# Output projection of the first block in two parts, the first between retention's steps

## The chip, the cores and the metric

The kernel runs on one core of a Trainium2 chip. A core has TensorE (PE, matrix products into PSUM), VectorE (DVE), ScalarE (ACT), GpSimd (POOL) and SyncE (SP, which issues most transfers), and they wait for each other by semaphores. The metric is the device time of one execution in microseconds (us); lower is better.

## The reference

All arithmetic is in float32: one sequence of 512 tokens, width 1024, runs through two layers of a first block, then through one layer of a second block that the change leaves alone. In each layer of the first block a mixer has three branches whose outputs are concatenated and projected:

```python
def hybrid_layer(x, ...):
    h = rms_norm(x, g_mix_pre)
    u = h @ w_in
    aq, ak, av, cu, rq, rk, rv, rg = jnp.split(u, SPLITS, axis=-1)
    y_att = chunk_attention(aq, ak, av, rel_bias)          # 384 wide, 6 heads
    y_conv = conv_module(cu, conv_w, conv_b, ...)          # 256 wide
    y_ret = retention(rq, rk, rv, rg)                      # 384 wide, 6 heads
    mix = jnp.concatenate([y_att, y_conv, y_ret], axis=-1) @ w_out   # 1024 x 1024
    x = x + rms_norm(mix, g_mix_post)
    h = rms_norm(x, g_mlp_pre)
    f = jnp.square(jax.nn.relu(h @ w_up)) @ w_down
    return x + rms_norm(f, g_mlp_post)
```

## The kernel before

Activations lie feature-major: a tile has 128 features on the partitions and the 512 tokens along it, so a width of 1024 is eight tiles. Each float32 operand is split into a high and a low part (`split`, `wload`: ACT rounds the high part, DVE subtracts), and a product is three products on PE, high by high, low by high, high by low (`mm3`). One unit of weights is 128 output features, 128 x 1024 numbers or 512 KB; 24 products of 512 columns belong to it. Units pass through three buffers `raw` for the load and four pairs `wh`, `wl` for the parts.

`gemm` takes units in turn. With `wide` = 4 its first four units advance together, with the contraction outermost, so that each input tile is used for four units as soon as it is there; later units go one by one. Behind each unit it may advance background work, written as generators: `pump_all` takes one or more steps of each.

`mixer` computes the input projection part by part in the order "card": convolution, attention, retention, gates. Behind the units of a part the branches run as background: a head of attention is a step of scores and softmax (eight score products on PE, of 512, 384, 256 and 128 columns, twice each) and a step of values; a head of retention the same without the softmax, with masks by POOL. In retention each pair of heads ends with a norm over 64 features: sums on PE against `hsel`, a reciprocal root on ACT and DVE, its broadcast by transposes on PE, two multiplications on DVE. The eight tiles `mix` are three of attention, two of convolution, three of retention. Then comes the output projection (wide 4) over all eight, whose results ACT copies out of PSUM (`e_out`); background work beside it is `bg2`, the projection of the second block's memory (products of 256 columns on PE, splits of its weights in halves of 512 columns). `post` takes the sum of squares, normalizes, adds to x and prepares the input of `mlp`, whose first gemm is again wide 4.

Nothing runs in the written order. `Plan` records every operation with a priority (its place, shifted by `ahead` or `filler`), and a list scheduler orders the recorded operations by a model of the engines' times and its slots (80 tiles `t`, 8 PSUM tiles `p`). `emit` then issues them in that order. So every instruction has the line of `emit` in the profile, L475, and groups are told apart by tile names: `p<-t,wh` and `p<-t,wl` are products with weights ("weight products" below), `p<-t` products of activations and of the memory, `p<-ident` transposes, `p<-ones` and `p<-hsel` sums over features.

## Time and profile before

| | us |
|---|---|
| median of 3 runs | 2514.57 |
| lowest and highest run | 2509.88, 2519.38 |
| span of the profiled execution, first to last instruction | 2510.5 |
| busy in it: PE, DVE, ACT, POOL | 2483.7, 1462.8, 946.0, 110.7 |

For the profiled execution the page gives its span and no other time. Matrix products are pipelined and their ends are modelled, so a busy PE may still be slowed by its clock or by loads of weights. The granted clock stands beside each stretch: 1.00 is 2.4 GHz, 0.50 is 1.2 GHz. The first layer's mixer ends and its up projection begins at about 280 us, the second layer's at about 913 us.

### The profile page before, as it was taken

What the parts mean: (1) busy time and instruction counts of PE and PEld (TensorE: products, weight loads), DVE (VectorE), ACT (ScalarE), POOL (GpSimd) and SP (SyncE); (2) the same over time, 40 slices, a digit from 0 to 9 for tenths busy, and PEclk for the clock granted to TensorE, in tenths of its full rate; (3) what the DMA queues carried; (4) which work ended last, traced back from release to release, by engine and by line L of the source; (5) the groups of instructions that cost most, each with busy time, mean ns of one, the idle gap of its engine ahead of it and who ended that gap; (6) DMA issues with size and microseconds to landing.
All of it is one profiled execution on the core that took longest, in us unless ns stands there. A gap on an engine that the chain in (4) does not pass through costs nothing.

```text
span 2510.5 us, 30038 instructions
## 1 busy us (share of the span) xinstructions
PE 2483.7 (99%) x11522; PEld 2033.4 (81%) x11522; DVE 1462.8 (58%) x2529; ACT 946.0 (38%) x1482; POOL 110.7 (4%) x214
## 2 busy tenths in 40 slices
PE   8999999999999999999999999999999999999998
PEld 7777888888887788788888888888878888888887
DVE  7985734545897579934565444456445555444445
ACT  4465532223346453322343222234455433322222
POOL 0011000000001100310000000000000000000000
PEclk9998999999999899999999999999999999999999
DMA  6441333233354234533313332265222243232232
GB/s 208 133 124 51 120 109 101 93 101 118 126 143 109 66 120 129 154 119 97 117 61 113 95 106 88 89 225 169 83 77 73 72 137 109 84 109 87 91 107 69
DMA packets 98160, 274.83 MB, mean 109 GB/s; under 512 B 13153, under 2 KB 20001, under 8 KB 98017
## 3 DMA queue, kind: packets, MB, share of 16 engines
q1 hardware_dynamic: 93184, 259.51, 33.1%
q0 software_dynamic: 4832, 13.41, 1.8%
q8 instruction: 90, 1.47, 0.2%
q14 instruction: 54, 0.43, 0.1%
HBM read 242.44 MB, written 19.94 MB: 105 GB/s over the span
## 4 chain that ended last, share of the span: by engine, by line
PE 95%; DVE 3%; ACT 1%; issue 1%; DMA 0%; POOL 0%; DVEq 0%; SPq 0%; ACTq 0%
PE p L475 95%; DVE t L475 2%; ACT t L475 1%; DVE wl L475 0%; ACT wh L475 0%; DMA raw<-in_mem_kv 0%; DVE s L475 0%; POOL t L475 0%; DMA t<-in_x 0%; ACT L475 0%; ACT s L475 0%; DVEq L1929 0%; SPq L475 0%; DVEq L475 0%; ACTq L475 0%
## 5 line engine op out<-in xcount | busy, mean ns | idle before, releaser
L475 PE MATMUL p<-t,wh 128*128 128x512 f32 (+1 forms) x6408 | 1994.4, 390 | 8.2 <-ACT wh L475 7.6
L475 PEld LDWEIGHTS p<-t,wh 128*128 128x128 f32 x6408 | 1201.8, 188 | 259.5 <-ACT wh L475 9.3
L475 PE MATMUL p<-t,wl 128*128 128x512 f32 x3204 | 1248.6, 390 | 1.2 <-DVE wl L475 1.1
L475 ACT ACTIVATE wh<-raw 128x1024 fp32r<-128x1024 f32 (+4 forms) x428 | 426.1, 1000 | 1203.4 <-PE p L475 802.1
L475 PEld LDWEIGHTS p<-t,wl 128*128 128x128 f32 x3204 | 603.3, 188 | 125.4 <-DVE wl L475 3.6
L475 DVE TENSOR_TENSOR wl<-raw,wh 128x1024 fp32r<-128x1024 f32 (+4 forms) x428 | 489.3, 1147 | 144.2 <-ACT wh L475 140.0
L475 DVE TENSOR_TENSOR t<-p,t 128x512 f32<-128x512 f32 (+5 forms) x388 | 238.4, 630 | 488.8 <-PE p L475 463.4
L475 DVE TENSOR_TENSOR t<-t 128x512 f32<-128x512 f32 (+10 forms) x688 | 360.0, 551 | 39.8 <-ACT t L475 32.3
L475 ACT ACTIVATE t<-t 128x512 f32<-128x512 f32 (+4 forms) x405 | 244.6, 617 | 124.9 <-DVE t L475 110.7
L475 PE MATMUL p<-t 128*128 128x256 f32 (+14 forms) x1200 | 233.8, 324 | 5.7 <-DVE t L475 3.6
L475 PEld LDWEIGHTS p<-t 128*128 128x128 f32 (+3 forms) x1200 | 165.5, 179 | 68.5 <-issue 28.6
L475 DVE TENSOR_TENSOR t<-t,p 128x512 f32<-128x512 f32 x104 | 71.7, 692 | 178.3 <-PE p L475 174.0
L475 ACT ACTIVATE t<-p 128x512 f32<-128x512 f32 (+7 forms) x290 | 130.2, 491 | 118.7 <-PE p L475 108.5
L475 DVE SCALAR_TENSOR_TENSOR t<-t,cols 128x512 fp32r<-128x512 f32 (+32 forms) x196 | 132.9, 712 | 4.3 <-ACT t L475 4.2
L475 DVE SCALAR_TENSOR_TENSOR t<-p,t 128x512 f32<-128x512 f32 (+1 forms) x84 | 57.4, 684 | 122.9 <-PE p L475 122.8
L475 ACT ACTIVATE t<-t,cols 128x512 fp32r<-128x512 f32 (+2 forms) x76 | 49.5, 671 | 29.4 <-DVE t L475 28.7
L475 PE MATMUL p<-ident,t 128*128 128x128 f32 x388 | 55.8, 281 | 1.3 <-DVE t L475 1.3
L475 ACT ACT_TABLE_LOAD x41 | 52.6, 1283 | 6.2 <-DMA t<-in_x 4.0
L475 PEld LDWEIGHTS p<-ident,t 128*128 128x128 f32 x388 | 46.9, 144 | 8.7 <-DVE t L475 1.7
L475 ACT ACTIVATE t<-t,s 128x256 f32<-128x256 f32 (+2 forms) x80 | 42.4, 531 | 19.6 <-DVE s L475 18.9
L475 DVE SCALAR_TENSOR_TENSOR t<-t 128x512 f32<-128x512 f32 (+1 forms) x72 | 45.0, 631 | 1.5
L475 DVE CUSTOM_DVE_ANT_0 t<-p,t 128x256 f32<-128x256 f32 (+2 forms) x80 | 34.5, 451 | 13.5 <-PE p L475 13.4
(57 smaller groups left out, 359.7 us busy)
## 6 DMA issues: line engine op xcount, KB each, us to landing
raw<-in_w_in SPq DMA_DIRECT2D x100, 512.0 KB, 3.7
raw<-in_f_in SPq DMA_DIRECT2D x88, 512.0 KB, 3.5
raw<-in_w_up SPq DMA_DIRECT2D x64, 512.0 KB, 3.5
raw<-in_w_down SPq DMA_DIRECT2D x64, 512.0 KB, 3.6
raw<-in_w_out SPq DMA_DIRECT2D x24, 512.0 KB, 3.6
raw<-in_f_down SPq DMA_DIRECT2D x32, 384.0 KB, 3.0
raw<-in_f_down SPq DMA_DIRECT2D x32, 320.0 KB, 2.8
t<-t SPq DMA_DIRECT2D x72, 128.0 KB, 2.3
```

Source lines behind the costliest of these rows:

```text
L475: fn(*args, **kw)
```

## The change

The output projection is done in two gemms. The first is over the first five tiles of `mix` (`EARLY = 5`: attention and convolution). It is recorded as soon as these five are there, one unit after the other, with one step of the remaining background (retention) behind each unit, and its results are copied from PSUM to `f` by ACT as before. The second, behind the last step of retention, is over the other three tiles, again one unit at a time, and DVE adds its results in PSUM to `f`. Each unit of weights is loaded in two pieces, 128 x 640 and 128 x 384. Products per unit are 15 and 9 in place of 24. The rest of the diff takes out comments and docstrings.

```diff
@@ -489,6 +489,7 @@
 
 
 TAIL, BACK = 4, 100
+EARLY = 5
 
 
 class Net:
...
@@ -1027,17 +1028,24 @@
 
         for i, kind in enumerate(self.ORDER):
             part(kind, 1 if i else 4)
+        while None in mix[:EARLY]:
+            self.pump_all(bg)
+
+        f = [None] * KT
+
+        def e_first(i, ps):
+            f[i] = self.T()
+            nc.scalar.activation(f[i], ps, AF.Copy)
+
+        def e_rest(i, ps):
+            nc.vector.tensor_tensor(f[i], f[i], ps, op=OP.add)
+
+        wo = d[f"w_out{l}"]
+        self.gemm([wo[i][:, :EARLY * P] for i in range(KT)], [self.split(m) for m in mix[:EARLY]], e_first, 1, bg,
+                  both=True)
         while bg:
             self.pump_all(bg)
-
-        f = [None] * KT
-
-        def e_out(i, ps):
-            f[i] = self.T()
-            nc.scalar.activation(f[i], ps, AF.Copy)
-
-        wo = d[f"w_out{l}"]
-        self.gemm([wo[i] for i in range(KT)], [self.split(m) for m in mix], e_out, 4, bg2, 1)
+        self.gemm([wo[i][:, EARLY * P:] for i in range(KT)], [self.split(m) for m in mix[EARLY:]], e_rest, 1, bg2, 1)
         self.finish(bg2)
         self.unpark()
         return self.post(f, f"norm_mix_post{l}", f"norm_mlp_pre{l}")
```

How the order moves, at three places. First PE in layer 0, behind the last unit of the gates. Rows are engine instructions by line, output and inputs, shape of the output, and how often one follows itself. Before, this is where the first weight product of the output projection stands, behind 64 rows of attention, retention and transposes:

```order
L475 MATMUL p<-t 128x256
L475 MATMUL p<-t 128x512
L475 MATMUL p<-t 64x512
L475 MATMUL p<-t 128x256
L475 MATMUL p<-t 128x128 x2
L475 MATMUL p<-t,wh 128x512
L475 MATMUL p<-t 128x384
L475 MATMUL p<-t 64x384
```

In the new order, six weight products come at the start of that stretch (here five rows between two heads' scores):

```order
L475 MATMUL p<-t,wh 128x512
L475 MATMUL p<-t,wl 128x512
L475 MATMUL p<-t,wh 128x512 x2
L475 MATMUL p<-t,wl 128x512
L475 MATMUL p<-t,wh 128x512
L475 MATMUL p<-t 128x512 x2
L475 MATMUL p<-t 128x384 x2
L475 MATMUL p<-t 128x256
```

and later each set of products of retention stands between weight products. Here the end of a set of values and the products behind it:

```order
L475 MATMUL p<-t 128x256
L475 MATMUL p<-t 64x256
L475 MATMUL p<-t 128x128
L475 MATMUL p<-t 64x128
L475 MATMUL p<-t,wh 128x512
L475 MATMUL p<-t,wl 128x512
```

So weight products moved from behind retention to between its sets. Second, PE in layer 0 between the output projection and the up projection, before, from the sums of squares (`ones`) over the transposes of the norm (`ident,s`, four) to the first product of the up projection:

```order
L475 MATMUL p<-ones,t 128x1 x6
L475 MATMUL p<-t 128x256 x12
L475 MATMUL p<-ones,t 128x1 x4
L475 MATMUL p<-t 128x256 x4
L475 MATMUL p<-ident,s 128x128 x2
L475 MATMUL p<-t 128x256 x7
L475 MATMUL p<-ident,s 128x128 x4
L475 MATMUL p<-t 128x256 x24
L475 MATMUL p<-t,wh 128x512
```

and now:

```order
L475 MATMUL p<-t,wh 128x512
L475 MATMUL p<-t 128x256 x32
L475 MATMUL p<-ones,t 128x1 x8
L475 MATMUL p<-t 128x256 x7
L475 MATMUL p<-ident,s 128x128 x4
L475 MATMUL p<-t 128x256 x9
L475 MATMUL p<-t,wh 128x512
```

The products of the memory (128x256) moved from behind the norm's transposes to ahead of them. Third, DVE in layer 0 at the same place, a part of its list ahead of the statistics of the norm (`TENSOR_SCALAR s<-p 128x4`). Before, it has the subtractions for weights (`wl`) and for the memory's weights (`t<-raw,t`) and the sums of squares (`t<-t`), and no additions out of PSUM:

```order
L475 TENSOR_TENSOR wl<-raw,wh 128x1024 x3
L475 TENSOR_TENSOR t<-t 128x512 x4
L475 TENSOR_TENSOR wl<-raw,wh 128x1024 x2
L475 TENSOR_TENSOR t<-t 128x512
L475 TENSOR_TENSOR wl<-raw,wh 128x1024
L475 TENSOR_TENSOR t<-raw,t 128x512 x2
L475 TENSOR_TENSOR t<-t 128x512
L475 TENSOR_TENSOR wl<-raw,wh 128x1024
```

and now, up to the statistics, with additions out of PSUM (`t<-t,p`) among them:

```order
L475 TENSOR_TENSOR t<-t,p 128x512
L475 TENSOR_TENSOR t<-raw,t 128x512
L475 TENSOR_TENSOR t<-t 128x512
L475 TENSOR_TENSOR t<-t,p 128x512
L475 TENSOR_TENSOR wl<-raw,wh 128x1024
L475 TENSOR_TENSOR t<-t 128x512
L475 TENSOR_TENSOR wl<-raw,wh 128x1024
L475 TENSOR_TENSOR t<-p,t 128x256
L475 TENSOR_TENSOR t<-raw,t 128x512 x2
L475 TENSOR_TENSOR t<-t 128x512
L475 TENSOR_TENSOR wl<-raw,wh 128x1024
L475 TENSOR_SCALAR s<-p 128x4
```

The eight additions joined the list that ends with the statistics.

## Rows read from the trace of the kernel before

**Rows 1.** The page: span, part 1 (busy us, share, instructions), part 4 (the chain).

```profile
span 2510.5 us, 30038 instructions
...
PE 2483.7 (99%) x11522; PEld 2033.4 (81%) x11522; DVE 1462.8 (58%) x2529; ACT 946.0 (38%) x1482; POOL 110.7 (4%) x214
...
PE 95%; DVE 3%; ACT 1%; issue 1%; DMA 0%; POOL 0%; DVEq 0%; SPq 0%; ACTq 0%
```

**Rows 2.** Windows: stretch and length, each engine busy (x), granted clock, DMA share, GB/s.

```profile
193.20:210.30 17.10, 16.99 (x46) 10.71 (x45) 5.62 (x13) 9.04 (x23) 4.26 (x16) 0.50 0.27 90
...
797.40:807.60 10.20, 9.43 (x23) 6.66 (x23) 6.73 (x25) 6.54 (x18) 1.72 (x5) 0.50 0.15 39
807.60:824.70 17.10, 17.10 (x78) 12.24 (x77) 13.07 (x29) 8.60 (x15) 2.75 (x5) 1.00 0.35 108
824.70:838.30 13.60, 13.60 (x34) 8.35 (x34) 4.09 (x11) 7.13 (x18) 4.15 (x16) 0.50 0.32 97
...
848.60:855.40 6.80, 6.80 (x21) 4.76 (x21) 2.72 (x5) 2.99 (x7) 1.61 (x6) 0.50 0.87 298
```

**Rows 3.** Windows: one head's score products twice, one head's value products.

```profile
166.73:169.35 2.62, 2.62 (x9) 1.29 (x7) 2.62 (x7) 2.34 (x5) 0.00 (x0) 1.00 0.23 53
195.12:199.62 4.50, 4.50 (x9) 2.28 (x8) 2.02 (x5) 1.75 (x4) 2.14 (x9) 0.50 0.35 117
210.22:211.62 1.40, 1.40 (x9) 1.22 (x10) 0.96 (x4) 1.35 (x4) 0.00 (x0) 0.98 0.00 0
```

**Rows 4.** Timeline of PE: start, length, instruction, count.

```profile
803.08 0.63 PE L475 MATMUL p<-t,wl 128*128 128x512 f32 x1
803.51 1.05 PE L475 MATMUL p<-t,wh 128*128 128x512 f32 x2
...
808.17 0.62 PE L475 MATMUL p<-t,wh 128*128 128x512 f32 x2
808.63 0.39 PE L475 MATMUL p<-t,wl 128*128 128x512 f32 x1
```

**Rows 5.** Timeline of PE: its waits beside retention, in brackets.

```profile
226.96 0.27 PE L475 MATMUL p<-t 128*64 128x128 f32 x1 [0.45 <-POOL t L475]
...
840.27 1.21 PE L475 MATMUL p<-t 128*128 128x512 f32 x5 [0.70 <-DVE t L475]
...
859.91 0.27 PE L475 MATMUL p<-t 128*64 128x128 f32 x1 [0.45 <-POOL t L475]
```

**Rows 6.** DMA issues: count, KB each, median us from issue to landing.

```profile
raw<-in_mem_kv SPq DMA_DIRECT2D x8, 512.0 KB, 4.0
```

**Rows 7.** Groups by form, ACT, 189 to 280 us: busy, mean ns, idle before.

```profile
L475 ACT ACTIVATE t<-t 128x512 fp32r<-128x512 f32 x4 | 2.5, 622 | 2.8 <-DVE t L475 2.8
```

**Rows 8.** Windows: last retention transposes to the up projection, both layers.

```profile
236.23:279.76 43.53, 43.30 (x230) 37.23 (x229) 22.18 (x36) 20.86 (x34) 0.74 (x1) 1.00 0.42 140
868.27:912.70 44.43, 43.76 (x228) 37.20 (x227) 21.84 (x32) 20.44 (x32) 1.09 (x2) 1.00 0.41 129
```

**Rows 9.** Timeline of PE around the same places in layer 0.

```profile
276.46 0.60 PE L475 MATMUL p<-ident,s 128*128 128x128 f32 x4
276.81 3.11 PE L475 MATMUL p<-t 128*128 128x256 f32 x24
279.76 0.40 PE L475 MATMUL p<-t,wh 128*128 128x512 f32 x1
```

**Rows 10.** Groups by form, DVE, 236 to 280 us.

```profile
L475 DVE TENSOR_TENSOR wl<-raw,wh 128x1024 fp32r<-128x1024 f32 x8 | 9.7, 1223 | 14.4 <-ACT wh L475 14.4
L475 DVE TENSOR_TENSOR t<-t 128x512 f32<-128x512 f32 x8 | 5.5, 689 | 2.0 <-ACT t L475 1.7
...
L475 DVE TENSOR_TENSOR t<-t,p 128x512 f32<-128x512 f32 x1 | 0.7, 686 | 1.4 <-PE p L475 1.4
L475 DVE TENSOR_TENSOR t<-p,t 128x256 f32<-128x256 f32 x1 | 0.4, 415 | 0.0
L475 DVE SCALAR_TENSOR_TENSOR s<-s 128x4 f32<-128x4 f32 x2 | 0.3, 162 | 0.1
```

## The prediction

> **What bounds the kernel now.** I read the page first. TensorE (PE) is busy 2483.7 of 2510.5 us and carries 95% of the chain that ended last; VectorE (DVE) carries 3% [rows 1]. The reader should see that no other engine has a claim on the end, so the change can gain in three ways only: PE waits less, its products take less time each, or there are fewer of them. The change keeps every product, so two ways are left.
>
> Then the stretches by granted clock [rows 2]. Where the last heads of attention and retention run and no weight product is there to go between, the clock is at 0.50, the lower of its two levels (1.2 of 2.4 GHz): 17.1 us in the first layer, 13.6 and 6.8 us in the second. PE is busy 16.99 of 17.10 us in the first of them, so this loss stands in no row of idle time. The stretch from 797.40 lies earlier, in the gate's products, and the change doesn't touch it.
>
> What the lower level costs is read from equal work at both. The eight score products of one head took 2.62 us at 1.00 and 4.50 us at 0.50 [rows 3]; a weight product took 0.43 us (803.08 to 803.51) against 0.23 us (808.17 to 808.63, two of them) [rows 4]. So about 0.42 of half-clock time is lost: 0.42 x 17.1 = 7.2 us in layer 0 and 0.42 x 20.4 = 8.6 us in layer 1, 15.8 us in all. That is the most that can be had from the clock.
>
> Real waits of PE beside retention are small. Three are long enough to count: 0.45 us on POOL in layer 0, and 0.70 on DVE and 0.45 on POOL in layer 1 [rows 5]. That is 1.6 us.
>
> **What the change adds at no cost.** Each layer gets 16 loads of weights (320 and 192 KB) for 8 of 512 KB, with the same bytes; a load of 512 KB, here one of the memory's, lands 4.0 us after issue [rows 6], and the weights are recorded 400 operations ahead of their use. Uncovered, a late one would cost up to that 4.0 once per layer. The eight copies by ScalarE (ACT) stay, but now run between retention's steps, where ACT has 0.62 us for one of 512 columns [rows 7] and some 35 us of room.
>
> **The clock, step by step.** The order of PE shows that the early products don't reach the whole half-clock stretch. They need attention's last pair of heads, and before that pair is done only six products (two of its five inputs) can be issued. The order before has 64 rows in a row without a weight product; the new one has 28 behind those six, and then 6, 33 and five times 15 weight products between retention's sets. Against before, one score set (4.50 us at half clock) and one set of value products (1.40 us at full clock [rows 3], an estimate of 2.8 at half) leave the stretch, and six weight products of 0.43 us enter it. So 17.1 - 7.3 + 2.6 = 12.4 us stay at half clock in layer 0, which gains 0.42 x 4.7 = 2.0 us. Layer 1's first dip goes from 13.6 to 8.9 us by the same sum (2.0), and its second dip, 6.8 us, lies where the weight products are now dense and goes altogether (2.9). The gain is 6.9 us, with bounds 0 (the dips last as long as now) and 15.8 (the six products lift the clock at once). I take the middle value by a row: at 797.40 the clock came back only at 807.60 [rows 2], although weight products ran from 803.08 at the latest [rows 4]. A few of them don't lift it at once. With the 1.6 us of waits the gains are **8.5 us**.
>
> **What the change takes away: the cover behind retention.** Before, all that waits for retention's last pair is hidden. From the broadcast transposes of the last norm (236.23) to the first product of the up projection (279.76) are 43.53 us [rows 8, 9], and 148 weight products at 0.23 us fill 34.0 of them. The other 9.5 us are memory products and norm work. DVE is busy for 22.18 us of the 43.53 and never in the way. After, only 49 weight products stand in that place (72 of the second part, 23 of them ahead of the transposes): 11.3 us. But DVE's list in it is as long as before. Counted in the new order from the multiplication by the broadcast to the statistics of the following norm, it has 9 additions or products out of PSUM at 0.69 (8 of them are new, the former copies of ACT), 8 of 512 columns at 0.69, 4 splits of 1024 columns at 1.22, 4 of 384 (no row; about 0.55 between 0.41 for 256 columns and 0.69 for 512), 4 splits of the memory's weights at the same 0.69, one of 0.41 and ten small ones at 0.16 [rows 10]: 6.2 + 5.5 + 4.9 + 2.2 + 2.8 + 0.4 + 1.6 = 23.6 us. Behind it comes the norm's own tail, 3.3 us from its transposes to the first up product (276.46 to 279.76); before, 24 memory products covered that tail, now 9 do in layer 0 and none in layer 1. Ahead of it, ACT's split of the last pair, 0.62 us [rows 7], holds the second part's last third.
>
> Upper bound per layer: 0.6 (the transposes) + 23.6 + 0.6 + 3.3 = 28.1 us; less 11.3 of weight products that leaves 16.8 against 9.5 now, a loss of 7.3. Lower bound, if DVE never leads: transposes, two multiplications and the split 2.6 us, then PE's own 11.3 + 48 memory products at 0.12 (24 in the 2.95 us from 276.81 to 279.76 [rows 9]) = 5.8, then 3.3 less what nine memory products cover, 1.1: 21.9 us, that is 10.6 against 9.5, a loss of 1.1. I take 5 us, nearer the upper end, since DVE runs its list in order and the statistics stand at its end. Layer 1 has the same items and as long a stretch, 44.43 us [rows 8]. Loss: **10 us** in both, with bounds 2 and 14.
>
> **The sum.** 10.0 - 8.5 = +1.5 us on a span of 2510.5. The runs' median, 2514.57, is 4.1 us above this span, and the span itself lies among the runs (2509.88 to 2519.38); I put the change on the median: 2514.57 + 1.5 = **2516 us**. What the planner reorders elsewhere I take as 0, with 2 to 3 us either way, since the count of products behind each of the stretches is the same.
>
> **Rivals.** (a) The clock stays up. If the six early products suffice to end each dip, 15.8 + 1.6 us are gained; with DVE's list partly overlapped (2.5 us lost per layer) the change is -12.4, or 2502 us. For it: from 807.60 to 824.70, where weight products stand between such sets, the clock is 1.00 throughout [rows 2]. Against it: the slow return at 797.40. (b) No gain from the clock: the dips end only when attention's last pair does, as now. Then +10.0 - 1.6 = +8.4: 2523 us. For it, the clock fell at 193.20 with PE busy all the time, and those score sets are still there. The Trainium skill ("TensorE: Matmul & The Clock Gate", Part 1, What's actually happening) has the gate follow how busy the engine has lately been, half rate being the state of an idle one. By that rule alone a PE that is never idle has no dip to cure, and the change gives nothing here. The trace disagrees on the cause (0.50 at 16.99 of 17.10 us busy), and the trace decides. (c) Slower: the weights behind DVE's list come late. Four loads for the up projection and two for the memory take turns in three raw buffers; a memory load lands after 4.0 us, and its two subtractions stand ahead of the norm's sums in DVE's queue. One turn is 4.0 + 1.24 (two splits by ACT) + 1.38 (two by DVE) = 6.6 us, and two turns can start once the second part's own raw buffers are free, some 10 us in (an estimate from the sums above): 23.2 us, just inside the list's 23.6. A third turn, for one load that waits, would put the end at 29.8 us, the first up product at 33.1, and the loss at 33.1 - 11.3 - 9.5 = 12.3 us per layer: 2514.57 + 24.6 - 8.5 = 2531 us. It decides once the list ends later than 28 us. Against it: the up loads are recorded far ahead, and DVE's order puts the memory's splits where the list has room for them.
>
> **Chances.** A measurement of this kernel tells 0.5%, 12.6 us, from no change. My forecast has 0.62, (b) 0.15, both inside that bound; (a) 0.12, at its edge and beyond; (c) 0.11. So faster 0.13, same 0.76, slower 0.11. The range takes in the bounds of the clock and of the cover without the two outer corners: 2503 to 2527 us.
>
> **What would show it.** Right: the clock falls near 193 and 825 as now, returns some 5 us sooner, and no dip remains near 849; from the last retention transposes to the first up product take about 26 us instead of 43.5, with PE waits of 2 us or more on DVE there. Wrong: a clock of 1.00 from 190 on (rival a), dips of 17 us (b), or PE waiting on DVE behind a late load (c). The prediction fails most easily in the 5 us per layer, which no row of before shows.

## The result: slower by 1.4%

| | before | after |
|---|---|---|
| median (lowest to highest), us | 2512.23 (2508.88 to 2519.38) | 2547.11 (2546.3 to 2552.95) |
| span of the profiled execution | 2510.5 | 2544.5 |

The ratio is 1.0143, 95% interval 1.0122 to 1.0164. Four runs stand behind each median. The page of the changed kernel, its lines for [rows 1]:

```profile
span 2544.5 us, 30163 instructions
...
PE 2493.4 (98%) x11522; PEld 2041.0 (80%) x11522; DVE 1473.9 (58%) x2561; ACT 950.8 (37%) x1498; POOL 106.4 (4%) x214
...
PE 94%; DVE 4%; ACT 1%; DMA 1%; issue 1%; SPq 0%; DVEq 0%; ACTq 0%
```

The same 11522 products, but DVE's share of the chain rose from 3 to 4% and transfers came in with 1%. The shares do not say where. For that, weight products are counted on PE's timeline: both kernels have the same 9612, so the n-th is the same place in the program, whatever moved around it. Each layer's place falls into three stretches: the **mixer** (from product 401, or 2701, to the last of the output projection, 792 or 3120), the **norm** (from there to the first up product) and the **up start** (from there to product 1001 or 3401). In us, from the two timelines:

| stretch | layer 0 before | after | | layer 1 before | after | |
|---|---|---|---|---|---|---|
| mixer | 161.2 | 163.9 | +2.7 | 176.3 | 175.2 | -1.1 |
| norm | 9.2 | 17.4 | +8.2 | 9.5 | 15.2 | +5.7 |
| up start | 48.6 | 57.4 | +8.8 | 65.0 | 73.1 | +8.1 |

These sum to 32.4 of the 34.0 us. The rest is below 1 us at any one place. So there are two losses in each layer, norm and up start, and next to no gain in the mixer. Windows over the changed kernel, first two in layer 0, the third in layer 1 (columns as in [rows 2]):

```profile
259.79:291.36 31.57, 25.98 (x133) 22.81 (x131) 24.53 (x45) 14.91 (x26) 0.75 (x1) 0.84 0.62 193
291.36:348.79 57.43, 52.69 (x221) 42.19 (x221) 42.82 (x65) 22.85 (x33) 0.55 (x1) 0.94 0.22 67
907.92:938.30 30.38, 22.97 (x126) 19.21 (x124) 24.63 (x46) 15.26 (x26) 2.16 (x4) 0.88 0.63 206
```

The first and third answer to [rows 8]: from the last retention transposes to the first up product take 31.6 and 30.4 us (26 were forecast; 43.5 and 44.4 stood before, with 99 and 103 weight products more in them). DVE is busy for 24.5 us of them, close to the 23.6 that were summed. PE is idle for 5.6 and 7.4 us, at a mean clock of 0.84 and 0.88.

**The norm stretch.** PE's timeline at the end of layer 0's mixer, with waits in brackets:

```profile
273.96 0.39 PE L475 MATMUL p<-t,wh 128*128 128x512 f32 x1
274.19 3.03 PE L475 MATMUL p<-t 128*128 128x256 f32 x24
280.15 2.59 PE L475 MATMUL p<-t 128*128 128x256 f32 x8 [2.94 <-ACT t L475]
282.54 3.41 PE L475 MATMUL p<-ones,t 128*128 128x1 f32 x16
...
287.45 1.06 PE L475 MATMUL p<-ident,s 128*128 128x128 f32 x4
288.15 1.93 PE L475 MATMUL p<-t 128*128 128x256 f32 x9
291.36 0.50 PE L475 MATMUL p<-t,wh 128*128 128x512 f32 x1 [1.27 <-ACT t L475]
```

DVE's timeline beside it:

```profile
275.20 0.68 DVE L475 TENSOR_TENSOR t<-t,p 128x512 f32<-128x512 f32 x1
275.90 1.23 DVE L475 TENSOR_TENSOR wl<-raw,wh 128x1024 fp32r<-128x1024 f32 x1
277.04 0.68 DVE L475 TENSOR_TENSOR t<-t 128x512 f32<-128x512 f32 x1
278.55 1.22 DVE L475 TENSOR_TENSOR wl<-raw,wh 128x1024 fp32r<-128x1024 f32 x1 [0.82 <-ACT wh L475]
279.69 0.42 DVE L475 TENSOR_TENSOR t<-p,t 128x256 f32<-128x256 f32 x1
280.13 1.29 DVE L475 TENSOR_TENSOR t<-raw,t 128x512 fp32r<-128x512 f32 x2
281.35 0.69 DVE L475 TENSOR_TENSOR t<-t 128x512 f32<-128x512 f32 x1
```

ACT's row for the memory's weights:

```profile
279.47 1.15 ACT L475 ACTIVATE t<-raw 128x512 fp32r<-128x512 f32 x2 [0.95 <-DMA raw<-in_mem_kv]
```

The last addition out of PSUM ends at 275.9; the norm's last sum runs at 281.35. Between them DVE does low parts of up weights and of the memory's weights, one of which waits for ACT, and PE spends 32 of the 48 memory products ahead of the norm's sums (`ones`). PE's wait of 2.94 us is for the memory's second load, issued at 274.70, which ACT rounds only at 279.47. After the norm's transposes only 9 are left, where before there were 24 [rows 9]. The Trainium skill ("PSUM — Partial Sum Buffer", Engine vs sequencer instructions) has the queues of ScalarE, VectorE and GpSimdE strictly first in, first out; the trace agrees, with one row's wait of 0.82 us holding the three groups behind it.

In layer 1 PE waits only 0.34 us for the memory's weights. There DVE has a low part of up weights, and its wait for ACT, within the norm itself, between the statistics and the reciprocal:

```profile
930.57 0.16 DVE L475 TENSOR_SCALAR s<-p 128x4 f32<-128x4 f32 x1 [0.82 <-PE p L475]
931.26 1.23 DVE L475 TENSOR_TENSOR wl<-raw,wh 128x1024 fp32r<-128x1024 f32 x1 [0.53 <-ACT wh L475]
...
932.74 0.17 DVE L475 RECIPROCAL s<-s 128x4 f32<-128x4 f32 x1
```

and PE, which has no memory product left there, waits at the norm's end:

```profile
938.30 0.80 PE L475 MATMUL p<-t,wh 128*128 128x512 f32 x1 [4.10 <-ACT t L475]
```

**The up start.** DVE's timeline in the kernel before, behind the statistics of the next norm:

```profile
301.72 3.50 DVE L475 TENSOR_TENSOR wl<-raw,wh 128x1024 fp32r<-128x1024 f32 x3 [0.47 <-ACT wh L475]
305.13 1.28 DVE L475 TENSOR_TENSOR t<-p,t 128x512 f32<-128x512 f32 x2
```

The same place in the changed kernel:

```profile
313.90 1.30 DVE L475 TENSOR_TENSOR t<-p,t 128x512 f32<-128x512 f32 x2 [2.42 <-PE p L475]
315.12 1.28 DVE L475 SCALAR_TENSOR_TENSOR t<-t 128x512 f32<-128x512 f32 x2
...
318.72 1.29 DVE L475 SCALAR_TENSOR_TENSOR t<-t 128x512 f32<-128x512 f32 x2
319.93 1.22 DVE L475 TENSOR_TENSOR wl<-raw,wh 128x1024 fp32r<-128x1024 f32 x1
```

And PE's timeline there:

```profile
316.89 0.50 PE L475 MATMUL p<-t,wh 128*128 128x512 f32 x1 [0.45 <-ACT wh L475]
321.20 0.79 PE L475 MATMUL p<-t,wl 128*128 128x512 f32 x1 [3.81 <-DVE wl L475]
```

Before, the low parts of the fifth to seventh up unit come first and the evictions of the first four units behind them. Now ten evictions (two in each of five rows, two of which are left out here) come first, and PE waits 3.81 us for the fifth unit's low part. Layer 1 has the same wait, 3.90 us.

**The clock.** Windows over stretches at half clock in the changed kernel, answering to [rows 2]:

```profile
197.40:200.80 3.40, 3.40 (x8) 2.20 (x8) 0.56 (x2) 3.37 (x9) 1.58 (x7) 0.50 0.03 5
207.60:214.40 6.80, 6.80 (x26) 5.94 (x25) 4.13 (x13) 3.58 (x7) 1.51 (x6) 0.50 0.00 1
279.30:289.50 10.20, 9.20 (x41) 8.91 (x42) 5.71 (x13) 2.41 (x4) 0.75 (x1) 0.50 0.67 206
320.30:327.10 6.80, 5.90 (x14) 4.64 (x15) 5.48 (x6) 1.43 (x2) 0.00 (x0) 0.50 0.56 154
842.50:859.60 17.10, 16.33 (x47) 11.06 (x47) 6.26 (x15) 9.39 (x24) 3.47 (x14) 0.50 0.01 3
934.70:941.50 6.80, 3.20 (x8) 2.50 (x9) 6.66 (x15) 3.61 (x6) 0.40 (x1) 0.50 0.48 179
```

In layer 0 the long dip of 17.1 us became 3.4 and 6.8 (12.4 were forecast), but new dips go with the two waits, 10.2 us at 279.30 and 6.8 at 320.30. In layer 1 the dip at 842.50 is longer than the 13.6 us before, and there is a new one at 934.70.

Waits and clock together account for the norm and up start stretches of both layers, which lost 30.8 us: PE is idle for 18.2 us more in them than before, and 27.2 us of them are at half clock, where before had none. At the 0.42 of the prediction that is 11.4 us (an estimate), so 29.6 in all. In every kernel below whose up start loses at most 0.3 us both are at nothing there, so in that stretch the clock's part goes with the waits.

### The profile page after: what moved, and what is told of

Same layout as the page of the kernel before. It is cut to its first block, busy times and chain, and to the rows that moved or that the text cites. A ratio compares the mean times of both kernels' runs of the same rounds, so it can differ in the third digit from the quotient of the medians.

```text
span 2544.5 us, 30163 instructions
## 1 busy us (share of the span) xinstructions
PE 2493.4 (98%) x11522; PEld 2041.0 (80%) x11522; DVE 1473.9 (58%) x2561; ACT 950.8 (37%) x1498; POOL 106.4 (4%) x214
## 4 chain that ended last, share of the span: by engine, by line
PE 94%; DVE 4%; ACT 1%; DMA 1%; issue 1%; SPq 0%; DVEq 0%; ACTq 0%
PE p L475 94%; DVE t L475 3%; ACT t L475 1%; DMA raw<-in_mem_kv 0%; DVE wl L475 0%; DMA t<-in_sa 0%; ACT wh L475 0%; DMA t<-in_x 0%; DVE s L475 0%; ACT L475 0%; SPq L475 0%; DVEq L1937 0%; ACT s L475 0%; ACTq L475 0%; DVEq L475 0%
## 5 line engine op out<-in xcount | busy, mean ns | idle before, releaser
L475 PEld LDWEIGHTS p<-t,wh 128*128 128x128 f32 x6408 | 1206.2, 189 | 274.8 <-ACT wh L475 12.1
L475 ACT ACTIVATE wh<-raw 128x1024 fp32r<-128x1024 f32 (+5 forms) x444 | 429.5, 971 | 1249.4 <-PE p L475 835.3
L475 DVE TENSOR_TENSOR wl<-raw,wh 128x1024 fp32r<-128x1024 f32 (+5 forms) x444 | 492.5, 1112 | 139.6 <-ACT wh L475 135.2
L475 DVE TENSOR_TENSOR t<-p,t 128x512 f32<-128x512 f32 (+6 forms) x388 | 237.4, 631 | 510.0 <-PE p L475 481.1
L475 DVE TENSOR_TENSOR t<-t 128x512 f32<-128x512 f32 (+11 forms) x688 | 358.1, 550 | 37.5 <-ACT t L475 29.3
L475 PE MATMUL p<-t 128*128 128x256 f32 (+12 forms) x1200 | 224.6, 318 | 8.2 <-DVE t L475 4.2
L475 DVE TENSOR_TENSOR t<-t,p 128x512 f32<-128x512 f32 x120 | 82.6, 691 | 180.9 <-PE p L475 176.4
L475 PEld LDWEIGHTS p<-ident,t 128*128 128x128 f32 x388 | 46.0, 143 | 11.4 <-DVE t L475 4.5
```

Of the source, the lines that this page charges most:

```text
L475: fn(*args, **kw)
```

## Experiments

The theory after this comparison: the norm stretch is long because its sums come late in DVE's queue (and the cover is gone), the up start because DVE's order flipped there. The main rival: the work that was added or left uncovered is too much in any order. The differences of the stretches against before, in us, are in one table behind the experiments.

**Order at the up start.** In `mlp`:

```diff
             def e_up(i, ps):
-                u = self.T()
+                with self.plan.ahead(-100 if c == 0 and i < 4 else 0):
+                    u = self.T()
...
```

> The changed kernel, but DVE takes the low parts of the fifth to seventh up unit's weights ahead of eight of the ten operations that evict the first four up units (it has them behind all ten now). Theory (the order of DVE's queue is the loss behind the first up product, 8.8 us in layer 0 and 8.1 us in layer 1): PE's waits of 3.8 and 3.9 us on DVE wl go, with the half-clock stretches behind them near 320 and 969, and the time falls by about 17 us to 2530. Rival (DVE has too much to do there in any order): the wait moves to another DVE row and the time stays within 5 us of the changed kernel's 2547.

2542.47 us, a ratio of 1.0102 (1.0074 to 1.0131). DVE's timeline in layer 0:

```profile
316.66 1.31 DVE L475 TENSOR_TENSOR t<-p,t 128x512 f32<-128x512 f32 x2 [2.41 <-PE p L475]
317.89 3.49 DVE L475 TENSOR_TENSOR wl<-raw,wh 128x1024 fp32r<-128x1024 f32 x3
321.29 1.29 DVE L475 SCALAR_TENSOR_TENSOR t<-t 128x512 f32<-128x512 f32 x2
```

PE no longer waits there in layer 0, and 1.2 us are left of 3.9 in layer 1. The up start fell from +8.8 and +8.1 to +1.5 and +3.5: the order is its cause, DVE had room. The whole gained less (the runs reach from 2531 to 2544): in the profiled execution the mixers were 1.7 and 3.2 us longer, and some 6 us more were lost outside the stretches. Layer 0's part of that is not the edit's, for PE, DVE, ACT and POOL have the order of the changed kernel up to 315 us.

**The memory's loads ahead.** In `mixer`, ahead of the first gemm:

```diff
+        bg.extend([g, 1] for g in bg2)
+        bg2.clear()
```

> The changed kernel, but the two units of the memory are loaded and split beside the first gemm, between retention's steps; their products remain fillers. Theory (the norm's last sum stands in DVE's queue behind the splits of a memory load that lands late, and PE falls to half clock while it waits): from the last retention transposes to the first up product take about 26 us in place of 31.6 and 30.4, the half-clock stretches near 279 and 935 go or shrink, the stretch behind the first up product keeps its loss, and the time falls by about 10 us to 2537. Rival (DVE's list itself sets the end, late load or not): the two stretches change by less than 2 us each and the time stays within 4 us of 2547.

2538.65 us, 1.0102 (1.0087 to 1.0117). The norm stretch fell from +8.2 to +2.6 in layer 0 but only from +5.7 to +5.3 in layer 1, and the half-clock stretches stayed (10.2 us at 281.2, 13.7 at 919.5). In layer 0 the norm's last sum starts 3.9 us behind the start of the last weight product in place of 7.4, so the late load and its splits are part of layer 0's loss, not of layer 1's. How much is not shown, since 28 of the 48 memory products moved into the mixer as well. 5.0 us came from layer 1's mixer, with 10.2 us at half clock in place of 27.3.

**The split alone, with the cover back.** The loop ahead of the first gemm becomes `while bg:`, so that both gemms stand behind retention; then the same with wide 4 in both.

> The split in two gemms alone: both are recorded behind retention's last step, as the one gemm was before. Theory (the loss ahead of the first up product is the lost cover, not the split): from the last retention transposes to the first up product take 43 to 46 us as before the change, no half-clock stretch lies there, the waits beside retention are those of before, and what remains is the loss behind the first up product, since DVE's list still has the evictions ahead of the weights there, some 17 us: about 2530. Rival (the split itself, its eight additions by DVE and twice as many loads, costs time): 50 us or more in each of these stretches, and 2540 or above.

> The split in two gemms alone again, both behind retention's last step, but with the first four units of each together (wide 4), as the one gemm was before. Theory (the split's late sums and the order they lead to, not the lost cover): 4 us per layer from the last weight product to the first up product as with wide 1, and a loss behind the first up product of 2 to 5 us, since one of the three low parts stands ahead of the evictions now; the clock beside retention as before the change; about 2525. Rival (with the width as before, the split costs nothing where cover is whole): all six stretches within 2 us of before, and 2515 or below.

2553.9 (1.0162, 1.0147 to 1.0177) and 2551.94 (1.0164, 1.0149 to 1.0179): no better than the changed kernel. 138 products stand behind layer 0's last retention transposes in the first of them, and the norm stretch is still +4.3 in both layers, the up start +10. So lost cover alone did not make the loss, and the theory had this wrong: of the norm's 8.2 and 5.7 us at most 3.9 and 1.4 came back with it. Layer 0's mixer was 10 us longer in both, with half-clock stretches of 17.1 us as before and a new one of 13.7 and 10.2 behind three waits of PE between 212 and 222 us. The mixer has 17.0 and 13.6 us more at half clock than before, 7.1 and 5.7 us by the 0.42, and the three waits are 2.5 us.

**Half of the units early.** Four units split, four whole behind retention:

```diff
-        self.gemm([wo[i][:, :EARLY * P] for i in range(KT)], [self.split(m) for m in mix[:EARLY]], e_first, 1, bg,
-                  both=True)
+        early = [self.split(m) for m in mix[:EARLY]]
+        self.gemm([wo[i][:, :EARLY * P] for i in range(4)], early, e_first, 1, bg, both=True)
...
-        self.gemm([wo[i][:, EARLY * P:] for i in range(KT)], [self.split(m) for m in mix[EARLY:]], e_rest, 1, bg2, 1)
+        late = [self.split(m) for m in mix[EARLY:]]
+        self.gemm([wo[i] for i in range(4, KT)], early + late, lambda i, ps: e_first(i + 4, ps), 4, bg2, 1)
+        self.gemm([wo[i][:, EARLY * P:] for i in range(4)], late, e_rest, 1, bg2, 1)
```

> Only the first four units of the output projection are split: their part over attention and convolution goes between retention's steps (60 products); the other four units stay whole behind retention (96 products), with the rest of the first four (36) behind them. Theory (cover): 110 products behind the last retention transposes leave PE without a wait above 1 us and without a half-clock stretch up to the first up product; the loss behind it stays, since DVE's list there still has the evictions first, 17 us; half of the gain beside retention, some 2 us, stays: about 2527. Rival (the loads and splits of the weights behind retention come late whatever is left there): a half-clock stretch near the first up product as in the changed kernel, and 2540 or above.

2562.14 us, 1.0192 (1.0176 to 1.0208), the worst of all but one: the norm stretches were +9.5 and +12.2, with 94 products behind layer 0's last retention transposes in place of 49. This speaks against cover again, though the order changed with it.

**The width alone.** The kernel before with `e_out, 1` in place of `e_out, 4`, run twice.

> The kernel before, one gemm over all eight tiles, but one unit at a time (wide 1) in place of four together. Theory now (the split, its late sums and the order that follows cost the time, and the width does not): as in the kernel before, the norm's transposes have 23 memory products behind them and DVE has the weights' low parts ahead of the evictions in layer 0; the three stretches of each layer (mixer up to its last weight product, from there to the first up product, behind it) stay within 3 us of before, and the time within 6 us of 2513. Rival (the width, which the change takes from 4 to 1 with the split, is the cause): half-clock stretches of 25 us and more beside retention as with both gemms behind it, and 2530 or above.

> The one gemm one unit at a time, again. Theory (the gain of 9.1 us in the second layer's mixer is the order's): faster than before by 3 to 9 us, an interval below 1. Rival (it was the clock's length of one execution): an interval that holds 1.

2504.16 us, 0.9972 (0.995 to 0.9993), and 2507.33, 0.9982 (0.9971 to 0.9993). The width, which the change took from 4 to 1 as well, is not what costs. This kernel beats both: five stretches stay within 0.7 us of before and layer 1's mixer is 9 us shorter in both profiles. It has 17.0 us at half clock in place of 30.7 there, which is 0.42 x 13.7 = 5.8 of the 9. How much of that is the width's is open: the medians gained some 8 and 3 us, and the kernel before with the sums first, below, has layer 1's mixer 5.2 us shorter too.

**Wide 4 in both gemms.**

> The changed kernel with wide 4 in both gemms. In the order, DVE has the weights' low parts ahead of the evictions again in layer 0, 83 and 84 up products stand ahead of the next norm's sums (85 and 84 before, 74 and 77 in the changed kernel), and 11 and 14 memory products stand behind the norm's transposes (24 and 16 before, 9 and none in the changed kernel). Theory (what costs is the order at the end of the mixer): no loss behind the first up product, 2 to 5 us per layer between the last weight product and the first up product, the gain beside retention stays at 0 to 6 us: about 2516. Rival (the lost cover and DVE's list, which the width does not change): 8 us and more per layer between the last weight product and the first up product, and 2530 or above.

2533.87 us, 1.0089 (1.0074 to 1.0105). The up start is that of before (+0.2 and 0.0), without any edit to it, and the norm stretch is not (+7.8 and +4.2). The two losses can be had apart, and the time is the rival's: the norm stretch did not go with the order at the up start. Layer 1's +4.2 is within the theory's 2 to 5, layer 0's +7.8 is not.

**Two edits together**, the first and second experiment.

> The changed kernel with the edits of the first two experiments together: the weights' low parts ahead of the evictions, and the memory's loads beside the first gemm. Theory (the two are separate losses): the stretch behind the first up product loses 1 to 3 us in layer 0 and 3 to 4 in layer 1 against before, the mixer keeps what the early loads gave, and the time is about 2525. Rival (they are one loss that moves): not below the better of the two, 2538.

2529.56 us, 1.0075 (1.0059 to 1.0092): below each of the two, as separate losses would have it, though 4.6 above the forecast.

**The additions.** First by POOL (`e_rest` copies with ACT, adds with `nc.gpsimd`), then left out, so that the output lacks the second part's sum with the first.

> The changed kernel, but the second part is copied out of PSUM by ACT and added to the first by POOL, so that DVE's list loses its eight additions per layer (5.5 us); PE's order there is the same row for row in layer 0. Theory (DVE's list with the eight additions holds the norm's sums): the stretch from the last weight product to the first up product, 17.4 and 15.2 us in the changed kernel, shortens by 3 to 5 us per layer, and the time falls to about 2539. Rival (a memory load that lands late holds them, whatever DVE adds): these stretches stay within 1.5 us, and the time within 4 us of 2547, or above it by what POOL takes longer.

> The changed kernel without its eight additions per layer: the second part is copied out of PSUM by ACT, as before the change, and goes on alone, so the sum with the first part is left out of the output. DVE's list is 5.5 us shorter, and no POOL operation of 1.6 us stands in its place, as it did where POOL added. Theory (DVE's additions hold the norm's last sum): the stretch from the last weight product to the first up product, 17.4 and 15.2 us, shortens by 3 us or more per layer; behind the first up product the order is that of the changed kernel, so its 8.8 and 8.1 us stay; about 2540. Rival (the memory's second load holds the sum): less than 1.5 us per layer, 2545 or above.

2556.21 (1.0179, 1.0164 to 1.0195) and 2549.21 (1.0149, 1.0132 to 1.0166). The first is a miss: an addition took POOL 1.3 to 1.7 us where DVE took 0.69, and the norm stretches grew to +12.1 and +12.7. The second shortened layer 0's norm stretch by 3.8 us and lengthened layer 1's by 2.3. The additions' 5.5 us alone are not the cause. Layer 0's 3.8 us are not clearly theirs either: its norm stretch has 2.0 us at half clock there and 10.2 in the changed kernel, which by the 0.42 is 3.4.

**The memory out of the mixer.** `run` passes no background to `mixer` and puts `memory_first` into the background of `mlp`.

> The changed kernel with the first two units of each layer's memory (loads, splits and products) taken out of the mixer and done as the first background work of the following mlp. Theory (the memory's loads and splits in DVE's queue ahead of the sums make the stretch long): the stretch from the last weight product to the first up product goes from 17.4 and 15.2 us to about 10, though nothing covers it now; the memory's 48 products cost their 5.9 us per layer in the mlp; the order has the weights' low parts ahead of the evictions and 81 and 79 products ahead of the sums, so the loss behind the first up product goes but for the memory's time. In all about 2525. Rival (DVE's additions and the norm's own length set the end): 14 us or more in that stretch, and 2535.

2563.3 us, 1.0206 (1.0191 to 1.0221). The norm stretches are the rival's: 17.4 and 17.1 us with no memory work in them. The time is 28 us above the rival's. Of that 13.5 us lie in the second block, between weight products 7050 and 7600: the planner moved 24 products of 128x512 from ahead of product 7250 to behind 7550, where 31 of 128x256 now stand as well; the changed kernel stands within 0.1 us of before there. PE's timeline in layer 0:

```profile
277.94 3.58 PE L475 MATMUL p<-ones,t 128*128 128x1 f32 x16 [5.15 <-DVE t L475]
282.81 1.12 PE L475 MATMUL p<-ident,s 128*128 128x128 f32 x4 [1.29 <-DVE s L475]
289.83 0.79 PE L475 MATMUL p<-t,wh 128*128 128x512 f32 x1 [5.90 <-ACT t L475]
```

DVE's timeline beside it:

```profile
273.04 0.68 DVE L475 TENSOR_TENSOR t<-t,p 128x512 f32<-128x512 f32 x1
273.64 1.22 DVE L475 TENSOR_TENSOR wl<-raw,wh 128x1024 fp32r<-128x1024 f32 x1
274.78 0.69 DVE L475 TENSOR_TENSOR t<-t 128x512 f32<-128x512 f32 x1
276.06 1.23 DVE L475 TENSOR_TENSOR wl<-raw,wh 128x1024 fp32r<-128x1024 f32 x1 [0.60 <-ACT wh L475]
277.20 0.68 DVE L475 TENSOR_TENSOR t<-t 128x512 f32<-128x512 f32 x1
```

Two things are left. Two low parts of up weights still stand between the last addition and the last sum. And from the end of that sum, 277.88, to the first up product are 12.0 us, the norm's own length with PE idle for most of it: with the memory's products its cover went too. So this run does not show that the order is the cause. That made the next experiment.

**The sums first.** One priority in the changed kernel:

```diff
-    def post(self, f, gname, nname):
+    def post(self, f, gname, nname, first=0):
...
-        rb = self.rms_r(f, out=False)
+        with self.plan.ahead(first):
+            rb = self.rms_r(f, out=False)
...
-        return self.post(f, f"norm_mix_post{l}", f"norm_mlp_pre{l}")
+        return self.post(f, f"norm_mix_post{l}", f"norm_mlp_pre{l}", 500)
```

> The changed kernel with one priority moved: the sums of the output projection's norm come in the queues as soon as they are ready, ahead of low parts of weights and of the memory's. In the order, 23 and 16 memory products stand behind the norm's transposes again (9 and none in the changed kernel, 24 and 16 before), 83 and 86 up products ahead of the next norm's sums, and the weights' low parts ahead of the evictions. Theory (one cause: the norm's sums come late in DVE's queue, the fillers are used up ahead of them, and the next norm then meets the evictions in the other order): both stretches at the end of each mixer go back, to 0 to 3 us above before each, and the time to about 2520. Rival (the additions and the splits are too much work for the cover that is left, in any order): 5 us or more per layer stay between the last weight product and the first up product, and 2530 or above.

2527.92 us, 1.0064 (1.0047 to 1.008). PE's timeline at the end of layer 0's mixer:

```profile
280.17 2.47 PE L475 MATMUL p<-t 128*128 128x256 f32 x16
283.36 2.44 PE L475 MATMUL p<-ones,t 128*128 128x1 f32 x16 [0.71 <-DVE t L475]
...
288.69 1.12 PE L475 MATMUL p<-ident,s 128*128 128x128 f32 x4 [0.77 <-DVE s L475]
289.46 3.88 PE L475 MATMUL p<-t 128*128 128x256 f32 x23
293.80 0.50 PE L475 MATMUL p<-t,wh 128*128 128x512 f32 x1 [0.46 <-ACT t L475]
```

DVE's timeline at the up start:

```profile
315.94 3.50 DVE L475 TENSOR_TENSOR wl<-raw,wh 128x1024 fp32r<-128x1024 f32 x3 [0.99 <-ACT wh L475]
319.35 1.28 DVE L475 TENSOR_TENSOR t<-p,t 128x512 f32<-128x512 f32 x2
```

One priority takes more than half of it back: with the sums first, 23 memory products stand behind the norm's transposes, DVE's order at the up start is that of before, and its loss goes from 16.9 to 0.5 us for both layers. The norm's loss goes from 13.9 to 8.6 us, not to the 0 to 3 a layer that were expected. In each norm stretch PE is idle for some 2 us more than before and 6.8 us are at half clock, up to 2.9 by the 0.42. That late sums are the one cause of both losses does not follow: with wide 4 in both gemms the up start was whole and the norm was not. Nor does the norm's loss follow the memory products behind its transposes: in layer 0 it is +2.6 with none of them (memory's loads ahead) and +4.6 with 23. The time is still 1.0064, and layer 0's mixer, +8.0, is in good part the clock's (last section). The same with wide 4, and on two kernels that are not split:

> The kernel with wide 4 in both gemms, and the sums of the output projection's norm moved ahead in the same way. Its order has 20 and 15 memory products behind the norm's transposes and the low parts ahead of the evictions. Theory (late sums): the 7.8 and 4.2 us between the last weight product and the first up product go to 0 to 3, and the time falls from 2534 to about 2522. Rival (too much work for the cover): less than 2 us per layer gained, 2530 or above.

> One gemm one unit at a time, as in the fastest kernel so far (2504), with the sums moved ahead too. Theory (late sums cost only where they are late, and they are not here): the stretches stay within 1.5 us of that kernel's, 2504. Rival (earlier sums give time in any kernel): 2500 or below.

> The kernel before with the sums moved ahead: a control. Theory: within 3 us of before, 2512, since the norm's tail is covered there already. Rival (the priority gives time in any kernel, and what it gives the changed one says nothing of late sums): 2505 or below.

2539.09 us (1.0112, 1.0095 to 1.0129), 2510.56 (0.9993, 0.9984 to 1.0002) and 2510.0 (0.9991, 0.9981 to 1.0001). The priority gives nothing clear of noise where the sums are not late; the second of the three came 6.6 us above its forecast of 2504, with layer 1's mixer 2 us longer than without the priority. With wide 4 it shortened the norm stretches (+7.8 to +3.7, +4.2 to +2.9), and yet the time did not fall: 2539 against 2534, from runs of 2532 to 2541. In the profiled execution 4.1 us of it lie in the second block, where the same 24 products moved as with the memory in `mlp`: it is 5.4 us shorter up to product 7250 and 9.5 longer behind 7550. The rest is open.

**What stays with the sums first**, the additions left out again:

> The changed kernel with the norm's sums first, and without its eight additions per layer: the second part goes on alone, and its sum with the first part is left out of the output. Theory (what stays once the sums come first is the additions on DVE): the 4.6 and 4.0 us that stay between the last weight product and the first up product go below 1.5 each. Rival (the splits of weights and memory, whose loads come late, hold it): 3 us or more stay per layer.

2535.36 us, 1.0098 (1.0084 to 1.0112). Layer 0's norm stretch went from +4.6 to +2.8. That these 1.8 us are the additions' is not shown: no half clock lies in the stretch here, and 6.8 us did with the additions, up to 2.9 us by the 0.42. In layer 1 the order came out another way (71 products ahead of the next sums, 86 with the additions), the up start lost 10.6 us with a wait of 4.36 on DVE `wl`, and nothing can be told of its norm stretch.

**The changed kernel again.**

> The changed kernel again, unchanged. Theory (its order costs what the stretches show): 2547 within 5 us, with the waits behind the first up product of 3.8 and 3.9 us in place. Open beside it: whether the half-clock stretches beside retention have the same lengths in a second profile (6.8, 3.4 and 6.8 us in layer 0) or reach the 30 us that two kernels with the same rows there showed.

2547.27 us, 1.0145 (1.013 to 1.0161), with waits of 3.82 and 3.90 us at the up starts: the losses come again with the order. The half-clock stretches beside layer 0's retention are 6.8, 3.4 and 3.4 us, so the lengths do change from one execution to the next.

The stretches of all, against before in us, and how many up products stand ahead of the next norm's sums in each layer (85 and 84 before). The changed kernel's own two rows differ by up to 1.1 us in a stretch, so less than that tells nothing, and mixers differ by more (last section):

| kernel | layer 0: mixer, norm, up start | layer 1: mixer, norm, up start | products ahead |
|---|---|---|---|
| changed | 2.7, 8.2, 8.8 | -1.1, 5.7, 8.1 | 74, 77 |
| changed again | 2.0, 7.1, 7.7 | -1.3, 5.0, 9.2 | 74, 77 |
| low parts first | 4.4, 7.3, 1.5 | 2.1, 5.1, 3.5 | 74, 70 |
| memory loads early | 2.2, 2.6, 9.7 | -6.1, 5.3, 9.4 | 75, 71 |
| both | 2.9, 3.9, 3.0 | -1.8, 5.1, 2.3 | 75, 76 |
| both gemms behind | 10.1, 4.3, 10.2 | 0.8, 4.3, 10.0 | 76, 75 |
| the same, wide 4 | 10.0, 5.9, 5.6 | 4.5, 7.5, 4.8 | 79, 81 |
| half early | 5.0, 9.5, 9.8 | 0.4, 12.2, 9.5 | 70, 70 |
| wide 4 in both | 2.8, 7.8, 0.2 | 3.3, 4.2, 0.0 | 83, 84 |
| added by POOL | 2.4, 12.1, 9.5 | -2.2, 12.7, 8.5 | 74, 70 |
| no additions | 7.8, 4.4, 9.6 | 1.4, 8.0, 8.9 | 74, 75 |
| memory in mlp | 1.9, 8.2, 2.7 | 7.1, 7.6, 7.6 | 81, 79 |
| sums first | 8.0, 4.6, 0.2 | -0.1, 4.0, 0.3 | 83, 86 |
| sums first, wide 4 | 6.4, 3.7, 0.1 | -1.6, 2.9, 0.1 | 85, 89 |
| sums first, no additions | 2.5, 2.8, 0.1 | -1.4, 4.2, 10.6 | 87, 71 |
| one gemm, wide 1 | -0.1, -0.4, 0.3 | -9.1, -0.7, 0.0 | 83, 84 |
| the same again | 0.6, -0.4, 0.3 | -9.0, -0.7, 0.0 | 83, 84 |
| the same, sums first | 0.8, -0.2, 0.1 | -7.2, -0.5, 0.0 | 83, 84 |
| before, sums first | 1.9, -0.4, 0.2 | -5.2, -0.5, 0.0 | 83, 84 |

The last column orders the up starts. Where 83 products or more stand ahead of the sums, the loss is at most 0.3 us; with 77 or fewer it is 7.7 to 10.6, unless the low parts are put first by hand; between them, 2.7 to 7.6. The likely reason, by the rows of DVE above, which no run tests by itself: if the norm's factor is there before the four units end, ten evictions are ready before the high parts that ACT has yet to round, and the list scheduler takes what is ready.

## Why the prediction was wrong

**Failed: "What the planner reorders elsewhere I take as 0, with 2 to 3 us either way, since the count of products behind each of the stretches is the same."** The count was the same and the order was not: 16.9 us of the 34 lie at the up starts, where the diff changes nothing. DVE's list was followed only up to the statistics of the output projection's norm.

**Mis-sized, and for the wrong reason: the cover, 10 us with bounds 2 and 14.** The norm stretches lost 13.9 us; with the mixers, mixer and norm together lost 10.9 and 4.6 us, against 2.5 and -1.1 by the sum (5 less the gains of 2.45 and 6.05). By the prediction's own reckoning, the stretch from the last retention transposes less 0.23 us a weight product, the term measured 10.8 and 9.6 us (with 9.5 before, as there), where it had 5 each and 7.3 at most. DVE's list was sized well (24.5 us busy against 23.6), and its end did lead, but waits stood in it, in layer 0 the sums on PE behind it ran at half clock, and the tail was 3.9 and 4.7 us in place of 3.3. The weight products that moved were not the main point: with them back, +4.3 us a layer stayed. The norm's sums stood behind work for later in an in-order queue, and PE spent its memory products ahead of them instead of behind. Of rival (c) the mechanism was right in layer 0, its splits ahead of the sums; its third turn of the raw buffers was not what happened (the memory's splits end 21.6 us into the stretch, where it had 23.2 for two turns and 29.8 for three), and it missed the time by 16 us.

**The clock, 6.9 us: not seen.** The dip in layer 0 shrank by 6.9 us, more than the 4.7 of the sum, and the dip near 849 did go. But layer 1's first grew, one of 3.4 in layer 0 became 6.8 beside a wait of 2.21 us on DVE that ends at 174.6, and the mixers gained 1.1 us at best. New dips of 30.6 us in all (10.2, 6.8, 3.4, 6.8 and 3.4, from 279.3 to 327.1 and from 910.8 to 972.2) lie at the ends of the mixers and in the up starts, beside the new waits; the sum had them nowhere, and they are some 11 of the 34 us by the estimate above. **The PE waits, 1.6 us** of gain, were more than taken back by that wait of 2.21 and one of 1.08.

**Right:** no wait of PE beside retention is on a load, and the second dip of layer 1 went. What stays open is the 4.6 and 4.0 us of the norm's stretch with the sums first, of which waits and half clock are the parts seen and their cause is not, and why the order with both gemms behind retention makes PE wait there.

## What to carry to other kernels

Where a scheduler orders the program, read its new order until it agrees with the old one again, not to the end of the edited lines: half of this loss lay behind that end, and a single priority took it away. An engine's queue runs in order, so ask of every row that sets an end what work for later stands ahead of it; here that decided the up starts and part of the norm's loss, and the amount of work or of cover alone explained neither. Fillers cover only a wait that comes while some are left: in layer 1 PE waited 4.10 us where none were.

## What was not expected of the hardware

The clock's dips differ between executions of the same order. The same rows of PE beside layer 0's retention, in the changed kernel and in the one with the sums first (PE, DVE, ACT and POOL have the same order in both up to 264 us):

```profile
178.20:244.80 66.60, 65.38 (x284) 49.59 (x283) 36.80 (x87) 39.81 (x84) 11.66 (x40) 0.91 0.15 46
```

```profile
179.10:249.60 70.50, 69.73 (x285) 52.32 (x284) 37.23 (x87) 40.23 (x85) 11.94 (x40) 0.83 0.15 43
```

66.6 against 70.5 us, with 10.2 and 23.9 us at half clock from 197 and 196 on; the same rows took 66.6 us where POOL added and 70.4 us without additions. In the changed kernel run again they took 64.6 us, with 6.8 us at half clock from 195 on. So up to 5.9 us of a mixer's difference can be the clock's alone, more than most of the mixer's differences in the table. The Trainium skill ("TensorE: Matmul & The Clock Gate", Part 1, What's actually happening) says that the stretch over which the gate looks runs freely and doesn't begin with the kernel. These two rows agree with that; no run here shows it by itself.
